# HGRN-2 values projected with tokens in the partitions, and the a-gate's product set beside the decays

## The chip, the core and the metric

The kernel runs on one core of a Trainium2 chip. A core has a matrix engine (TensorE, PE in the profile), which multiplies a stationary tile with a moving one into a PSUM bank, three engines for elementwise work (VectorE = DVE, ScalarE = ACT, GpSimd = POOL) and SyncE (SP), which starts DMA transfers. Each engine runs its own list of instructions in order; semaphores join them. The metric is the time of one execution on the device, in microseconds, the median of the runs. Loads of stationary tiles are a row of their own (PEld), which overlaps PE.

## What is computed

One layer of a diffusion backbone, for 1152 tokens (1024 latents and 128 context tokens) of width 1024. A normalised and modulated input goes through one input projection, `w_in`, whose columns feed two token mixers: HGRN-2 with four heads of 128, and RWKV-7 with eight heads of 64. An output projection and a gated ConvFFN follow. The change touches two places of the mixers:

```
def hgrn2_mixer(u_a, lb, norm_w, s0):
    q, i, zf, zb, g = jnp.split(u_a, 5, axis=-1)
    q = heads(jax.nn.silu(q))
    i = heads(i)
    f_f = lb[0] + (1 - lb[0]) * jax.nn.sigmoid(zf)
    f_b = lb[1] + (1 - lb[1]) * jax.nn.sigmoid(zb)
    o_f, S_f = hgrn2_chunk_scan(q, heads(1 - f_f), i, heads(jnp.log(f_f)), s0[:, 0])
...
def rwkv7_mixer(u_b, p, s0):
    u_b = dwconv1d(u_b, p['rwkv_conv'])
    r, k, v, wdf, wdb, ad, gd = jnp.split(u_b, idx, axis=-1)
    w_f = jnp.exp(-DECAY_SCALE * jax.nn.sigmoid(p['rwkv_w0'][0] + jnp.tanh(wdf) @ p['rwkv_w2'][0]))
    w_b = jnp.exp(-DECAY_SCALE * jax.nn.sigmoid(p['rwkv_w0'][1] + jnp.tanh(wdb) @ p['rwkv_w2'][1]))
    a = jax.nn.sigmoid(p['rwkv_a0'] + ad @ p['rwkv_a2'])
    kk = heads(k * p['rwkv_k_k']).astype(jnp.float32)
    k = k * (1 + (a - 1) * p['rwkv_k_a'])
```

`i` holds the HGRN-2 values, taken as they are, while q, both forget gates and g go through a nonlinearity. `a` is the a-gate of RWKV-7, `w_f` and `w_b` are its decays; each of the three is a product of inner size 32.

## The kernel before

**Products in three parts.** Inputs are fp32. The modulated input lies in SBUF as `hh` (rounded) and `hl` (the rest), with the 1024 channels in 8 groups of 128 partitions (`KT`) and the 1152 tokens in the columns. A weight column block is loaded into `wr` (512 KB; one buffer), `split` makes `wh` (a cast on ACT) and `wl` (the difference, on DVE; for the heads both carry the line of the call, L1229), and `proj` computes wh·hh + wh·hl + wl·hh: for each of three blocks of 384 tokens, 8 x 3 matmuls (L1070, L1071, L1072) of 128 stationary columns (the weights) by 384 moving ones (the tokens) into one of two banks, "pj". So a result has channels in its partitions and tokens in its columns. There are two buffers of `wh` and two of `wl`.

**HGRN-2's projections** (`hgrn_in`, L1225 to L1250): for each head in turn the blocks f, b, q and i, and at the end g of all heads. f, b, q and g go through Tanh to tiles "ha" and "hb" (two buffers each) and by DMA to DRAM. The value branch, `which == "i"`, turns the result round, since the scan needs tokens in the partitions: copy from the bank (L1234), three 128x128 transposes on PE (L1238) into another "pj" bank, copy again (L1239) and one store of 192 KB to `d_hv` (L1240). The scan loads the values of three token tiles from there at L1550 and L1650.

**RWKV-7's features** (`features`, from L1309, once for each of four head pairs, each in three blocks of 384 tokens): per block the a-gate's product from rows 64 to 95 of `wlora` and `twt` (`small_proj`, L1299, called at L1328) into a bank "sp", Tanh on ACT (L1331), the a-gate's use in `nb` and `k`; then the bonus sums (L1343), transposes of the values (L1353), and after these the two decays' products from rows 0 to 31 and 32 to 63 (L1364) into two banks "sp", with the decays' work behind them; last the products of pairs (L1397, L1398). Tag "sp" has two banks. Tag "el" has four places of 256 columns in the last two banks, and is used by `elim`.

**The eliminations** (`elim`, L1431): five of them, one behind each pair's features and one over all pairs; 31 steps of two DVE instructions each (L1441, L1444), then 32x32 products on PE (L1462, L1464). DVE does other work between the steps. The RWKV scan (its first product is L1713), the HGRN scan (L1582, L1608, L1627 and others), the output projection and the FFN (L2065, L2229) follow.

**What sets the order.** The Python code only records operations into a `Plan`. `close` finds what each depends on. Three tables written out in the file then decide: `SEQUENCE` the order in which the operations are issued (each engine's list is its part of it), `ENGINE_OF` the engine of every operation that has a choice (copies, combinations, stores: V, A, G, S), and `PLACE_OF` which buffer each tile takes. The remaining HGRN projections are spread by this order between the eliminations and into the scan.

## Time and profile before

| | |
|---|---|
| three runs | 1771.46, 1771.28, 1767.26 us; median 1771.28 |
| profiled execution | 1769.48 us, its span 1767.7 |
| TensorE clock granted, mean | 0.998 |
| DMA, whole span | 352.97 MB moved, mean 200 GB/s |
| start, to 40 us | loads, modulation, first columns |
| 40 to 487 us | projections, RWKV features, the eliminations |
| 487 to about 840 us | both scans, with projections between |
| about 840 to 1010 us | rest of the scans, output projection |
| 1010 to 1515 us | FFN up and its convolution |
| 1515 to 1768 us | FFN down |

The bounds of the stages are read from the lines that run in them. In the profile, "L1070 PE MATMUL banks<-hh,wh 128*128 128x384 f32 x768 | 278.5, 363 | 4.4" reads: line, engine, operation, tile written and tiles read, stationary tile (rows by columns), output (partitions by elements), count; then busy us and mean ns of one; then the idle time of the engine ahead of it, and what released it. A matmul's duration there reaches from its start to its modelled end, and consecutive ones overlap. `banks` is PSUM; `fx`, `low` and `top` are regions of SBUF that hold several tiles in turn ("ha", "hb" and `wlora` lie in `fx`, `twt` in `low`), so one name stands for several tiles.

### The profile page before, as it was taken

Reading aid. Unit: us, or ns where it says so; the run is one execution under the profiler, and the core shown is the slowest. Engines: PE = TensorE matmul, PEld = TensorE weight load, DVE = VectorE, ACT = ScalarE, POOL = GpSimd, SP = SyncE. Lnnn points to the kernel's source line nnn. Section 1 sums busy time; section 2 is a strip of 40 time slices with the busy share of each in tenths; the row PEclk is TensorE's granted clock in tenths of the full one; section 3 lists DMA queues with packets and bytes.
Section 4 is the critical chain, followed back from the end, with each engine's and each line's share of the span. In section 5 each row is a group of like instructions: output and inputs, shape, how many; then the busy total and the mean of one; then the engine's idle time right before and its main releaser. Section 6 shows DMA issues by size and latency. Waiting matters only on the chain.

```text
span 1767.7 us, 44608 instructions
## 1 busy us (share of the span) xinstructions
PE 1708.6 (97%) x17726; PEld 1539.8 (87%) x17726; DVE 1434.8 (81%) x2742; ACT 936.8 (53%) x1955; POOL 350.5 (20%) x543
## 2 busy tenths in 40 slices
PE   6999999999999999999999999999999999999998
PEld 4888888888988888888778899999999999878787
DVE  5648889977779988886879797888988888878766
ACT  5657576663255656664556764444444444554542
POOL 0003141352222011112110122232333322000000
PEclk9999999999999999999999999999999999999999
DMA  8426365486777788989997757777877777896775
GB/s 278 137 72 164 89 162 139 112 232 195 203 207 221 212 246 278 288 271 289 296 288 264 215 122 153 155 157 160 165 156 153 146 162 149 282 306 218 229 231 183
DMA packets 342068, 352.97 MB, mean 200 GB/s; under 512 B 73180, under 2 KB 264565, under 8 KB 341508
## 3 DMA queue, kind: packets, MB, share of 16 engines
q1 hardware_dynamic: 287508, 282.27, 53.0%
q0 software_dynamic: 54352, 67.85, 19.6%
q8 instruction: 139, 2.28, 0.5%
q14 instruction: 69, 0.57, 0.1%
HBM read 254.99 MB, written 118.10 MB: 211 GB/s over the span
## 4 chain that ended last, share of the span: by engine, by line
PE 55%; DVE 18%; DMA 15%; issue 5%; ACT 4%; SPq 1%; POOL 1%; DVEq 0%; ACTq 0%; POOLq 0%
PE banks L2065 14%; PE banks L1070 6%; PE banks L1072 5%; PE banks L1071 5%; PE banks L2229 5%; DVE low L2153 3%; DMA low<-in_ffn_w_up_dram 2%; DMA wr<-in_ffn_w_down_dram 2%; PE banks L1955 1%; PE banks L1957 1%; PE banks L1956 1%; DMA d_t<-in_ffn_w_down_dram 1%; DMA low<-d_a 1%; DMA wr<-in_ffn_w_up_dram 1%; DMA wr<-d_o 1%
## 5 line engine op out<-in xcount | busy, mean ns | idle before, releaser
L1070 PE MATMUL banks<-hh,wh 128*128 128x384 f32 x768 | 278.5, 363 | 4.4 <-DVE fx L1250 3.1
L1072 PE MATMUL banks<-hh,wl 128*128 128x384 f32 x768 | 257.8, 336 | 0.0
L1071 PE MATMUL banks<-hl,wh 128*128 128x384 f32 x768 | 257.5, 335 | 0.0
L2153 DVE SCALAR_TENSOR_TENSOR low<-low,pf 128x1024 f32<-128x1024 f32 x176 | 225.4, 1281 | 7.9 <-ACT low L2147 5.2
L2065 PE MATMUL banks<-qm,wh 128*128 128x320 f32 x968 | 224.1, 310 | 0.2 <-ACT fx L2102 0.2
L2065 PE MATMUL banks<-hbm,wh 128*128 128x256 f32 x880 | 164.4, 283 | 3.6 <-DVE low L2123 1.9
L2065 PE MATMUL banks<-qm,wl 128*128 128x320 f32 x528 | 162.9, 308 | 0.2 <-DVE wl L2035 0.2
L1070 PEld LDWEIGHTS banks<-hh,wh 128*128 128x128 f32 x768 | 144.3, 188 | 20.5 <-issue 8.5
L2065 PEld LDWEIGHTS banks<-qm,wh 128*128 128x128 f32 x968 | 160.7, 189 | 0.5 <-ACT fx L2102 0.4
L1071 PEld LDWEIGHTS banks<-hl,wh 128*128 128x128 f32 x768 | 144.6, 188 | 2.7 <-issue 1.4
L1072 PEld LDWEIGHTS banks<-hh,wl 128*128 128x128 f32 x768 | 144.2, 188 | 0.0
L2065 PEld LDWEIGHTS banks<-hbm,wh 128*128 128x128 f32 x880 | 139.1, 190 | 5.2 <-DVE low L2123 2.5
L2065 PE MATMUL banks<-ham,wh 128*128 128x256 f32 (+1 forms) x616 | 132.0, 294 | 0.0
L2065 PE MATMUL banks<-hbm,wl 128*128 128x256 f32 x440 | 124.4, 283 | 0.6 <-DVE wl L2035 0.6
L2102 ACT COPY fx<-banks 128x256 f32<-128x256 f32 (+1 forms) x132 | 52.1, 398 | 108.1 <-PE banks L2065 101.3
L2065 PEld LDWEIGHTS banks<-ham,wh 128*128 128x128 f32 x616 | 101.5, 190 | 0.1
L2065 PEld LDWEIGHTS banks<-qm,wl 128*128 128x128 f32 x528 | 99.1, 188 | 0.6 <-DVE wl L2035 0.6
L2065 PEld LDWEIGHTS banks<-hbm,wl 128*128 128x128 f32 x440 | 83.9, 191 | 0.8 <-DVE wl L2035 0.8
L2173 POOL DMA_DIRECT2D d_t<-in_ffn_w_down_dram x44 | 45.0, 1050 | 183.9 <-DMA d_t<-d_t 139.9
L2035 ACT CAST wh<-wr 128x512 fp32r<-128x512 f32 x73 | 45.2, 622 | 66.2 <-PE banks L2065 28.6
L2035 ACT CAST wh<-low 128x512 fp32r<-128x512 f32 x81 | 50.0, 620 | 52.9 <-PE banks L2065 25.5
L2065 PE MATMUL banks<-ham,wl 128*128 128x256 f32 (+1 forms) x264 | 77.0, 292 | 0.0
(578 smaller groups left out, 4369.3 us busy)
## 6 DMA issues: line engine op xcount, KB each, us to landing
wr<-in_w_in_dram SPq DMA_DIRECT2D x34, 512.0 KB
d_t<-in_ffn_w_down_dram POOLq DMA_DIRECT2D x61, 256.0 KB, 5.8
low<-d_a SPq DMA_DIRECT2D x53, 256.0 KB
low<-d_ak SPq DMA_DIRECT2D x64, 192.0 KB
low<-d_kb SPq DMA_DIRECT2D x36, 256.0 KB
low<-in_ada_w_dram SPq DMA_DIRECT2D x32, 256.0 KB
fx<-in_ada_w_dram SPq DMA_DIRECT2D x16, 512.0 KB
top<-in_ada_w_dram SPq DMA_DIRECT2D x16, 512.0 KB
```

The lines of the kernel that those rows point to most:

```text
L1070: mm(o, wh[:, kt, :], hh[:, kt, c], kt == 0, False)
L1071: mm(o, wh[:, kt, :], hl[:, kt, c], False, False)
L1072: mm(o, wl[:, kt, :], hh[:, kt, c], False, kt == KT - 1)
L1955: mm(ps, oh[:, kt, :], woh, kt == 0, False)
L1956: mm(ps, oh[:, kt, :], wol, False, False)
L1957: mm(ps, ol[:, kt, :], woh, False, kt == KT - 1)
L2035: split(*w, src)
L2065: pe.matmul(o, a[:, kt, :], b[:, kt, :], start=start and first, stop=last, skip_group_check=not start)
L2102: act.copy(keep[n], y[:, 0:w])
L2153: dve.scalar_tensor_tensor(av, shifted(dy, dx), tap(3 * dy + dx), av, MUL, ADD)
L2173: acc(td[j][k], b)
L2229: pe.matmul(o, x, y, start=fresh and f, stop=l, skip_group_check=not fresh)
```

## The change

Four parts.

- The HGRN-2 values are projected by a new function, `hgrn_rows`, for two heads at a time: the tokens are the stationary side (128 columns of `hh` or `hl`) and the weights of two heads the moving one (256 columns), so the result has tokens in its partitions. It takes nine token tiles of 8 x 3 matmuls (L1242, L1243, L1244 of the changed file). The weights come in two halves of four channel groups each, so that they fill both `wh` and both `wl` buffers. A result is copied from its bank once (L1246) and stored in two parts of 64 KB (L1248). The copies and transposes of the old branch are gone.
- The a-gate's product is taken in two halves of 192 columns into tag "el", and stands in one group with the two decays' products, at the start of the block (L1353, L1356); its Tanh goes in two halves as well (L1358).
- `close` counts what every alternative form of an operation reads, not the first alone, and the places of tag "el" may be taken in any order.
- The three tables are new throughout.

```
+    def hgrn_rows(h):
+        ws = []
+        for k0 in (0, 4):
+            raw = tl("wr", [P, 4, 256])
+            ld(raw, w_in[k0 * P:(k0 + 4) * P, 512 + h * P:512 + h * P + 256].rearrange("(a p) n -> p a n", p=P))
+            ws.append((tl("wh", [P, 4, 256], F32R), tl("wl", [P, 4, 256], F32R)))
+            split(*ws[-1], raw)
+        for i in range(NT):
+            o, c = pbank()[:, 0:256], slice(i * P, (i + 1) * P)
+            for kt in range(KT):
+                wh, wl = ws[kt // 4]
+                with plan.together():
+                    mm(o, hh[:, kt, c], wh[:, kt % 4, :], kt == 0, False)
+                    mm(o, hl[:, kt, c], wh[:, kt % 4, :], False, False)
+                    mm(o, hh[:, kt, c], wl[:, kt % 4, :], False, kt == KT - 1)
+            t = tl("hb", [P, 256])
+            copy(t, o)
+            for j in range(2):
+                st(hvd[h + j][:, i, :], t[:, P * j:P * j + P])
...
         for which in parts:
+            if which == "i":
+                hgrn_rows(h)
+                continue
...
-                if which == "i":
-                    copy(ta, ps)
-                    pv = pbank()
-                    with plan.together():
-                        for j in range(3):
-                            pe.transpose(pv[:, j * P:(j + 1) * P], ta[:, j * P:(j + 1) * P], ident)
-                    copy(tb_, pv[:, 0:384])
-                    st(hvd[h][:, 3 * tb:3 * tb + 3, :], tb_.rearrange("p (a b) -> p a b", b=P))
-                    continue
...
-            ps = small_proj(wlora[64:96, cb], twt[64:96, c])
-            act.activation(ta, ps, AF.Tanh, scale=0.5, bias=dp[:, D_A0H + p:D_A0H + p + 1])
+            dec = [pbank("sp")[:, 0:384] for d in range(2)]
+            al = [pbank("el", 256)[:, 0:192] for i in range(2)]
+            with plan.together():
+                for d in range(2):
+                    mm(dec[d], wlora[32 * d:32 * d + 32, cb], twt[32 * d:32 * d + 32, c], True, True)
+                for i in range(2):
+                    t0 = tb * 384 + 192 * i
+                    mm(al[i], wlora[64:96, cb], twt[64:96, t0:t0 + 192], True, True)
+            for i in range(2):
+                act.activation(ta[:, 192 * i:192 * i + 192], al[i], AF.Tanh, scale=0.5,
+                               bias=dp[:, D_A0H + p:D_A0H + p + 1])
...
-            dec = [pbank("sp")[:, 0:384] for d in range(2)]
-            with plan.together():
-                for d in range(2):
-                    mm(dec[d], wlora[32 * d:32 * d + 32, cb], twt[32 * d:32 * d + 32, c], True, True)
...
-    hin = iter([(h, w) for h in range(4) for w in "fbqi"] + [(h, "g") for h in range(4)])
+    hin = iter([(h, w) for h in range(4) for w in ("fbqi", "fbq")[h % 2]] + [(h, "g") for h in range(4)])
...
-        for m, a, k, _ in forms[0][1]:
-            w, r = self.operands(m, a, k)
-            writes += w
-            reads += r
+        for n, (_, l) in enumerate(forms):
+            for m, a, k, _ in l:
+                w, r = self.operands(m, a, k)
+                writes += [] if n else w
+                reads += r
...
-    plan.tag("el", [(mp, 512 * 6 + 256 * b) for b in range(4)], 256)
+    plan.tag("el", [(mp, 512 * 6 + 256 * b) for b in range(4)], 256, True)
...
-0 12 13 14 11 2 15 16 27 1 17 18 19 4 20 22 28 29 33 3 24 30 39 23 31 32 34 35 36 40 37 38
+11 27 28 29 0 1 17 12 2 30 18 19 33 39 13 14 15 20 4 3 16 21 22 23 24 25 31 32 34 35 36 37
```

The order on PE around the a-gate, in the second token block of the fourth head pair, before: the a-gate's product (L1299) stands by itself among projection matmuls and products of an elimination (L1462), with a group of transposes of the old value branch (L1238) two rows behind it; the names `wh_133` and `wl_136` are weight buffers with their numbers.

```order
L1072 MATMUL banks<-hh,wl_136 128x384
L1299 MATMUL banks<-low,fx 128x384
L1462 MATMUL banks<-top 32x32 x16
L1238 MATMUL banks<-c_ident,fx 128x128 x3
L1070 MATMUL banks<-hh,wh_133 128x384
```

The decays of the block (L1364) come 94 rows later, behind the transposes of the RWKV values, also among projections. In the changed kernel the products of a block stand in one group, here those of the same block, among matmuls of the new value projection (L1242 to L1244):

```order
L1242 MATMUL banks<-wh_133,hh 128x256
L1243 MATMUL banks<-wh_133,hl 128x256
L1244 MATMUL banks<-wl_136,hh 128x256
L1353 MATMUL banks<-low,fx 128x384 x2
L1356 MATMUL banks<-low,fx 128x192 x2
L1242 MATMUL banks<-wh_134,hh 128x256
```

The a-gate has moved into the decays' group, as two products behind two; the decays have moved ahead of the bonus sums and the transposes.

The order on PE where the first block of new value products begins: the last three matmuls of a projection of the old form (L1074 to L1076 are `proj` in the changed file) read weight buffers `wh_133` and `wl_136`, and twelve of the new form on the other two buffers follow, of which the first and the last three are shown; then comes the first that reads `wh_133` again, with other contents.

```order
L1075 MATMUL banks<-hl,wh_133 128x384
L1076 MATMUL banks<-hh,wl_136 128x384
L1242 MATMUL banks<-wh_134,hh 128x256
...
L1242 MATMUL banks<-wh_134,hh 128x256
L1243 MATMUL banks<-wh_134,hl 128x256
L1244 MATMUL banks<-wl_135,hh 128x256
L1242 MATMUL banks<-wh_133,hh 128x256
```

Before, a projection on the one pair of buffers ran for 72 matmuls while the other pair was filled; now both pairs are read in turn until nine token tiles are done.

The order on PE between the products of the fourth elimination and those of the fifth, before: 16 products of the fourth (L1464), a group of transposes, and then projections, the first of 240 in a row; further on the 16 first products of the fifth (L1462) stand ahead of another group of transposes.

```order
L1072 MATMUL banks<-hh,wl_136 128x384
L1464 MATMUL banks<-top,fx 32x32 x16
L1238 MATMUL banks<-c_ident,fx 128x128 x3
L1070 MATMUL banks<-hh,wh_134 128x384
...
L1072 MATMUL banks<-hh,wl_136 128x384
L1462 MATMUL banks<-top 32x32 x16
L1238 MATMUL banks<-c_ident,fx 128x128 x3
L1070 MATMUL banks<-hh,wh_133 128x384
```

In the changed kernel the last products of the fourth (L1488) are followed by projections of the old form, and those of the fifth (L1486) stand inside the second block of the new form:

```order
L1486 MATMUL banks<-top 32x32
L1488 MATMUL banks<-top,fx 32x32 x17
L1074 MATMUL banks<-hh,wh_134 128x384
...
L1244 MATMUL banks<-wl_135,hh 128x256
L1486 MATMUL banks<-top 32x32 x16
L1242 MATMUL banks<-wh_133,hh 128x256
L1243 MATMUL banks<-wh_133,hl 128x256
```

Between the two sets of products 240 matmuls of 384 columns have become 216 of them and 120 of 256 columns, and the transposes are gone.

55 lines of the change are left out of this document (28 added, 27 removed), and 602 rows, old and new, of the table SEQUENCE.

## The prediction

> **What bounds the kernel now.** I read the page's first part, then the busy times cut at four places of the program, then the chain of waits of one stretch, then single rows of the timeline.
>
> ```profile
> PE 1708.6 (97%) x17726; PEld 1539.8 (87%) x17726; DVE 1434.8 (81%) x2742; ACT 936.8 (53%) x1955; POOL 350.5 (20%) x543
> core 0: us, PE busy (x) PEld busy (x) DVE busy (x) ACT busy (x) POOL busy (x), PEclk, DMA share, GB/s
> 0.00:40.00 40.00, 24.38 (x156) 17.77 (x156) 21.35 (x61) 23.40 (x48) 4.09 (x20) 0.96 0.85 277
> 40.00:487.00 447.00, 439.16 (x4540) 395.05 (x4539) 351.19 (x715) 255.87 (x523) 116.39 (x218) 1.00 0.57 152
> 487.00:840.00 353.00, 340.09 (x6671) 300.27 (x6665) 295.65 (x734) 201.44 (x482) 62.72 (x120) 1.00 0.84 251
> 840.00:1010.00 170.00, 163.79 (x1597) 136.85 (x1594) 140.78 (x280) 101.83 (x222) 18.38 (x32) 1.00 0.86 271
> 1010.00:1515.00 505.00, 499.58 (x3716) 495.65 (x3716) 437.18 (x644) 235.35 (x458) 146.48 (x151) 1.00 0.74 156
> 1515.00:1768.00 253.00, 241.59 (x1064) 194.22 (x1062) 188.62 (x312) 118.88 (x228) 2.47 (x3) 0.99 0.73 238
> ```
>
> PE is busy in 98% of 40 to 487 us (projections, RWKV features, eliminations) and in 96% of 487 to 840 (scan, with the remaining HGRN projections as filler). The clock is full, so nothing is to be had there. The change works in these two stretches; the FFN and what follows it have the same products before and after, and I move them by nothing. DVE is second everywhere: 79% of the first stretch, 84% of the second, with 57 us idle in the latter. A busy PE is not a bound PE, so the second stretch is asked what its chain runs over.
>
> ```profile
> by line: PE banks L1070 7.4%; PE banks L1072 6.0%; PE banks L1071 5.9%; DVE top L1608 4.9%; PE banks L1627 4.3%; PE banks L1713 4.2%; DVE top L1607 4.2%; PE banks L1582 4.0%; PE banks L1767 3.7%; PE banks L1784 3.4%; PE banks L1760 3.4%; is
> L1070 PE MATMUL banks<-hh,wh 128*128 128x384 f32 x192 | 73.8, 384 | 0.0
> ```
>
> The three projection lines hold 19.3% of that chain, 68 us of 353. They issue 3 x 192 = 576 matmuls there, which at the interval below take 100 us. So about 68% of a filler matmul is on the path, and I count what leaves this stretch at 0.68.
>
> **The prices.** The mean of a matmul row (384 ns) is its latency; what the PE pays is the interval between starts.
>
> ```profile
> 440.12 0.33 PE L1071 MATMUL banks<-hl,wh 128*128 128x384 f32 x1
> ...
> 445.84 0.33 PE L1071 MATMUL banks<-hl,wh 128*128 128x384 f32 x1
> 1505.75 0.40 PE L2065 MATMUL banks<-hbm,wh 128*128 128x256 f32 x2
> ...
> 1507.19 0.40 PE L2229 MATMUL banks<-ham 128*128 128x512 f32 x1
> ```
>
> 33 intervals of 384 columns in 5.72 us are 0.1733 us each; 12 of 256 columns in the FFN, same type and a new stationary tile each time as in the new projection, take 1.44 us, 0.120 each.
>
> The value projection had 288 matmuls of 384 columns, 49.9 us, and gets 432 of 256, 51.8 us: **+1.9 us** for the same columns. The Trainium skill ("TensorE: Matmul & The Clock Gate", section "Back-to-back issue gap") gives N / 2.4 + 2.5 ns, by which the two forms would cost 46.8 and 47.2 us, so +0.4 as an estimate; the rows are 11 ns over it at both widths and decide.
>
> ```profile
> 343.81 0.49 PE L1238 MATMUL banks<-c_ident,fx 128*128 128x128 f32 x3
> 344.06 0.42 PE L1070 MATMUL banks<-hh,wh 128*128 128x384 f32 x1
> 344.32 0.33 PE L1071 MATMUL banks<-hl,wh 128*128 128x384 f32 x1
> 107.67 0.91 PE L1299 MATMUL banks<-low,fx 32*128 32x384 f32 x2
> 108.51 0.44 PE L1070 MATMUL banks<-hh,wh 128*128 128x384 f32 x1
> 108.79 0.34 PE L1071 MATMUL banks<-hl,wh 128*128 128x384 f32 x1
> 346.68 0.91 PE L1364 MATMUL banks<-low,fx 32*128 32x384 f32 x4
> 347.52 0.44 PE L1070 MATMUL banks<-hh,wh 128*128 128x384 f32 x1
> ```
>
> A group of three transposes holds the PE 0.25 us and stretches the next interval from 0.17 to 0.26: 0.34. At its other end stands the latency, 0.5; I take 0.45, since the matmul ahead is stretched too. Twelve groups go: -5.4 us.
>
> One a-gate product holds the PE 0.84 us and stretches the next interval to 0.28, so 0.94; twelve go, **-11.3 us**. The pair of decays takes 0.84 as well, as much as the one product alone, so products in different strips of 32 rows already run side by side. The a-gate's rows 64 to 95 are a third strip. Its two halves of 192 columns take half of 0.84 each, so both fit behind the decays: cost 0, between 0 and one half left over, 0.42 x 12 = 5.0. The Trainium skill (same page, section "The mechanism") says that matmuls start and end strictly in program order. By it a second half that waits for its strip may also hold back what follows, which is the upper end; no run here shows three strips at once.
>
> **Where they fall.** By the order of instructions, before and after: up to the last pair product of the features (381 us) the PE loses 75 projection matmuls (-13.0), 3 groups of transposes (-1.4) and all a-gate products (-11.3), and gets 216 value matmuls (+25.9): +0.2. From there to the first scan product (487 us) it loses 141 (-24.4) and 5 groups (-2.3) and gets 216 (+25.9): -0.8. Behind it 72 matmuls (-12.5) and 4 groups (-1.8) are missing: -14.3, at 0.68 **-9.7 us**.
>
> The middle piece isn't read from its sum, because two eliminations on DVE pace it.
>
> ```profile
> L1444 DVE TENSOR_TENSOR top<-top 128x31 f32<-128x31 f32 (+15 forms) x31 | 10.7, 344 | 1.0
> L1441 DVE TENSOR_TENSOR top<-top 128x31 f32<-128x31 f32 (+15 forms) x31 | 10.6, 343 | 0.9
> 420.81 1.08 PE L1462 MATMUL banks<-top 32*32 32x32 f32 x32
> 432.77 0.55 PE L1238 MATMUL banks<-c_ident,fx 128*128 128x128 f32 x3
> 475.10 0.63 PE L1462 MATMUL banks<-top 32*32 32x32 f32 x16
> 487.46 0.71 PE L1713 MATMUL banks<-low 64*128 64x128 f32 x8
> ```
>
> The fourth elimination fills 383 to 418 us on DVE: 21.3 us of its own, the rest other work between its steps (the two rows are of that stretch). Then come its products, the fifth elimination and its products. Filler ahead of the fourth's products: 198 matmuls before, 162 now, 6.2 us less, but DVE isn't faster, so I expect PE idle there instead: between -6.2 and 0, taken at 0. Inside its products 33 matmuls go: -5.7. Between them and the fifth's products (432.8 to 475.1 us) PE never pauses; 240 matmuls and a transpose group become 216 and 120 of the new ones: +37.4 +14.4 -41.6 -0.5 = +9.7. Inside the fifth's products 48 and two groups become 96 new ones: +11.5 -8.3 -0.9 = +2.3. Sum between +0.1 and +6.3. The upper end has DVE on the path; I take +2.5, below the middle of 3.2, since a DVE with less between its steps can end earlier.
>
> **What the new form adds.** Its weights lie in both weight buffers for nine token tiles. Where the first block of it begins, the second buffer has just been read by the last matmul of the old form.
>
> ```profile
> L1229 ACT CAST wh<-wr 128x1024 fp32r<-128x1024 f32 x20 | 21.0, 1048 | 6.1 <-PE banks L1071 3.3 <-DMA wr<-in_w_in_dram 2.7
> L1229 DVE TENSOR_TENSOR wl<-wr,wh 128x1024 fp32r<-128x1024 f32 x20 | 24.6, 1230 | 2.6 <-ACT wh L1229 2.4
> DMA to landing us min/median/max: 2.7/3.3/5.4
> L1234 ACT COPY fx<-banks 128x384 f32<-128x384 f32 x12 | 5.8, 480 | 20.6 <-PE banks L1072 16.6 <-DVE top L1441 4.0
> L1331 ACT ACTIVATE top<-banks,dp 128x384 f32<-128x384 f32 x12 | 6.9, 577 | 5.9 <-PE banks L1299 5.9
> ```
>
> Cast and difference take 2.3 us; 12 matmuls on the first buffer cover 1.4 of it. The wait is +0.8, with everything behind it on the in-order PE; at the second block 18 matmuls (2.2 us) come first, about 0. Bounds 0 to 3 for both, if ACT or DVE are late. At the end of both blocks the order puts other products or matmuls on the freed buffer first.
>
> A result tile is copied (some 0.4 us) and stored by two DMAs instead of one larger one; such stores landed in 3.3 us. With two tiles and a token tile every 24 x 0.12 = 2.9 us a tile has 5.8 us, so this hides: 0. If landing goes to its 5.4 us, each of 18 tiles is late by about 1 us; that end (+10, where the PE has nothing else) I give little weight, since both blocks have other products between.
>
> ACT loses 24 copies of 0.48 (11.5 us) and gets 16 smaller ones; its a-gate function goes in two calls of 192 columns instead of one of 0.577 us. ACT was half idle in both stretches, which hides this. Start, FFN and end keep their work: 0, within 3 either way, as their order is new too.
>
> **Sum** against the profiled execution's 1769.5 us (span 1767.7): +0.2 +0.8 +2.5 -9.7 = -6.2, so **1763 us**. The median of the three runs is 1771.3, 1.8 above that execution; I predict on the execution's scale.
>
> **The rivals.**
>
> *The scan stretch doesn't follow the PE.* Its chain also runs over the scan's own steps and DVE (L1607, L1608). If the filler only sat in gaps, -9.7 becomes about -2, and the time is 1771. Against it speaks the share of the projections on the chain, for it that PE waits were short but many. The same time comes out if the a-gate's halves aren't hidden (+5.0).
>
> *More comes through.* If all 14.3 us of the scan stretch and the -6.2 of the fourth elimination's filler count: 1763 - 4.6 - 8.7 = 1750.
>
> *Slower: DVE sets the pace.* The new order gives DVE more copies of the scan stretch.
>
> ```profile
> L1579 DVE COPY top<-top 128x384 f32<-128x384 f32 x12 | 4.3, 360 | 0.8 <-PE banks L1582 0.4 <-ACT top L1553 0.4
> L1817 DVE COPY top<-banks 64x256 f32<-64x256 f32 x12 | 5.0, 418 | 0.9 <-PE banks L1786 0.7
> ```
>
> L1579 goes from 12 to 20 there (+2.9), L1817 from 12 to 19 (+2.9), with L1601, L1762, L1769 and L1728 and less of L1628 some 10 us in all. If DVE is the limit, the scan stretch gets nothing from the PE and up to 10 us more; with the middle piece at +6.3 and the wait at 3 the time is 1769.5 + 0.2 + 3 + 6.3 + 10 = 1789 at most, 1779 with half of the copies on the path and the rest as in the sum. It decides once more than about 10 of DVE's 57 idle us lie where the scan can't use them. Against it: these are waits that mostly end on PE in the rows.
>
> **Chances.** Forecast (1757 to 1766) 0.47, more 0.12, no release or no hiding (within 0.3%, 1766 to 1776) 0.27, slower by DVE 0.14. A measurement of this kernel tells 0.3%, 5.3 us, from no change. A part of the forecast's own case lies near the edge, so: faster 0.57, same 0.28, slower 0.15. The range takes in the larger gain and the case without release, and leaves out a tenth on either side: 1750 to 1777; the likeliest case alone is 1757 to 1766.
>
> **What will show it.** Right: the new product's rows 0.12 us apart; the rows of the decays and the a-gate's halves within 0.9 us together; the first scan product at 487 to 493 us; the stretch from there to the FFN's first product 7 to 13 us shorter. Wrong: scan products not earlier against their first one, DVE above 90% there, or PE waiting for a weight split or a store at the new product's lines. A different length of the FFN or of the end by more than 3 us would mean that the new order matters more than the change of work.

## The result, and the profile after

The change made the kernel slower. The changed kernel takes 1786.05 us, median of five runs (1778.66 to 1788.16), against 1768.11 (five runs, 1765.78 to 1771.46) of the kernel before in the same session: ratio 1.0089, 95% interval 1.0071 to 1.0107 (the comparison's own estimate, not the quotient of the medians, which is 1.0101). The forecast was 1763 with a range of 1750 to 1777. The profiled execution took 1784.69 us (span 1782.9) at a mean granted clock of 0.991, against 1769.48 (1767.7) at 0.998.

The page's first part and the busy times cut at the same places as before (the columns are those of the table in the prediction):

```profile
PE 1708.3 (96%) x17858; PEld 1546.3 (87%) x17858; DVE 1437.5 (81%) x2779; ACT 915.1 (51%) x1931; POOL 375.5 (21%) x592
40.00:487.00 447.00, 429.85 (x4503) 392.52 (x4502) 346.20 (x717) 245.86 (x515) 121.50 (x233) 0.98 0.55 148
487.00:840.00 353.00, 326.84 (x6360) 286.57 (x6360) 286.72 (x711) 185.84 (x448) 77.65 (x144) 0.98 0.77 231
1515.00:1768.00 253.00, 253.00 (x1164) 208.94 (x1163) 201.64 (x329) 129.97 (x247) 8.05 (x12) 1.00 0.78 253
```

PE is as busy as before in all (1708), but in a longer span. The stretches are cut at the same times in both kernels, so they don't hold the same work. In the first two, PE has lost 9 and 13 us of busy time and the clock is no longer full. In the last one PE is never idle (253.0 of 253); before, it idled 11.4 us there, of which 6.8 lie behind its last product of FFN down.

Where the difference of 15.2 us arises is read from the first and last start of five lines that both kernels have: products of pairs (L1398, now L1422), first products of the RWKV scan (L1713, now L1737), first products of the output projection (L1955, now L1979), FFN up (L2065, now L2089), FFN down (L2229, now L2253). The view of one line gives the durations of a matmul (minimum, median, maximum, ns), then the first and last start. Before:

```profile
L1398 PE MATMUL banks<-top x576: 192/193/215, 137.9 to 381.3; 64*32 64x32 f32 x192
L1713 PE MATMUL banks<-low x576: 272/272/374, 487.5 to 923.8; 64*128 64x128 f32 x192
L1955 PE MATMUL banks<-ham,wh x72: 389/389/504, 869.7 to 994.8; 128*128 128x512 f32 x72
L2065 PE MATMUL banks<-qm,wh x968: 305/309/414, 1006.3 to 1505.5; 128*128 128x320 f32 x194
L2229 PE MATMUL banks<-qm x165: 277/392/499, 1515.2 to 1760.9; 128*128 128x512 f32 x153, 128*128 128x256 f32 x12
```

After:

```profile
L1422 PE MATMUL banks<-top x576: 186/193/259, 139.0 to 394.5; 64*32 64x32 f32 x192
L1737 PE MATMUL banks<-low x576: 272/272/419, 507.0 to 954.6; 64*128 64x128 f32 x192
L1979 PE MATMUL banks<-ham,wh x72: 389/389/504, 900.5 to 1021.4; 128*128 128x512 f32 x72
L2089 PE MATMUL banks<-qm,wh x968: 305/310/412, 1032.2 to 1525.4; 128*128 128x320 f32 x194
L2253 PE MATMUL banks<-qm,ham x78: 278/395/403, 1591.8 to 1775.2; 128*128 128x512 f32 x66, 128*128 128x256 f32 x12
```

| piece | before | after | difference | forecast |
|---|---|---|---|---|
| to the last product of pairs | 381.3 | 394.5 | +13.2 | +1.0 (+0.2, and 0.8 for the wait) |
| from there to the scan's first product | 106.2 | 112.5 | +6.3 | +2.5 (upper end +6.3) |
| from there to the FFN's first product | 518.8 | 525.2 | +6.4 | -9.7 |
| from there to the last product of FFN down | 754.6 | 743.0 | -11.6 | 0 |
| rest of the span | 6.8 | 7.7 | +0.9 | 0 |

Three pieces came out longer than the sum had them, and the FFN, which the sum left alone, came out shorter. The traces below show that two kernels with the same instructions in a piece can differ there by 8 to 10 us, so each difference is no better than that of two traces.

The prices that the sum was made of are confirmed, in the changed kernel's timeline of PE (start, duration, line, shape, count). The new value product, from the first block's start:

```profile
339.93 0.28 PE L1242 MATMUL banks<-wh,hh 128*128 128x256 f32 x1
...
340.88 0.28 PE L1244 MATMUL banks<-wl,hh 128*128 128x256 f32 x1
```

Eight intervals in 0.95 us are 0.119 each (forecast 0.120). The group of decays and a-gate halves:

```profile
103.54 0.33 PE L1076 MATMUL banks<-hh,wl 128*128 128x384 f32 x1
103.80 0.59 PE L1353 MATMUL banks<-low,fx 32*128 32x384 f32 x2
103.82 0.59 PE L1356 MATMUL banks<-low,fx 32*128 32x192 f32 x2
104.23 0.49 PE L1353 MATMUL banks<-low,fx 32*128 32x384 f32 x2
104.25 0.48 PE L1356 MATMUL banks<-low,fx 32*128 32x192 f32 x2
104.66 0.45 PE L1074 MATMUL banks<-hh,wh 128*128 128x384 f32 x1
```

The group holds the PE 0.86 us, the decays alone held it 0.84: the halves are hidden. Nor is the first value block's wait far off: PE waited 0.6 us for the difference on DVE there (forecast 0.8).

What the forecast did not have is the clock. Before, the granted clock halves only at the start and the end; after, it does so six times between 200 and 830 us, 27.3 us in all. The changed kernel's busy times, cut at the steps of the clock around the end of the fourth elimination:

```profile
421.59:425.00 3.41, 3.30 (x20) 2.98 (x18) 3.07 (x11) 0.00 (x0) 0.00 (x0) 1.00 0.90 282
425.00:428.42 3.42, 1.25 (x45) 1.09 (x49) 3.42 (x4) 0.93 (x3) 0.00 (x0) 0.99 0.01 2
428.42:431.83 3.41, 2.39 (x148) 2.11 (x143) 3.31 (x6) 1.87 (x4) 0.00 (x0) 0.50 0.32 120
431.83:435.24 3.41, 2.82 (x97) 2.61 (x86) 1.75 (x3) 0.00 (x0) 0.67 (x1) 0.50 0.55 154
435.24:438.66 3.42, 3.42 (x13) 3.42 (x12) 0.09 (x1) 0.56 (x1) 1.78 (x3) 0.51 1.05 269
```

What PE waited for in the second of these windows, in the view of waits (engine, tile and line, what it waited for, us in total, times, longest):

```profile
PE banks L1486 <- DVE top L1471: 1.4, 1, 1.4
PE banks L1486 <- ACT top L1497: 0.8, 1, 0.8
```

PE runs out of filler ahead of the products (L1486), waits 1.4 and 0.8 us, is busy 1.25 of 3.42 us, all of it in 32 x 32 products of the elimination, and gets half the clock for the next 10.24 us. A projection matmul then starts every 0.32 us (435.43, 435.75) instead of 0.17. The price of all six, in time of PE itself, is at most half of 27.3 us, since PE was not busy throughout.

### The profile page after: what moved, and what is told of

It reads as the page before. It is cut to its first block, busy times and chain, and to the rows that moved or that the text cites. A ratio compares the mean times of both kernels' runs of the same rounds, so it can differ in the third digit from the quotient of the medians.

```text
span 1782.9 us, 44799 instructions
## 1 busy us (share of the span) xinstructions
PE 1708.3 (96%) x17858; PEld 1546.3 (87%) x17858; DVE 1437.5 (81%) x2779; ACT 915.1 (51%) x1931; POOL 375.5 (21%) x592
## 4 chain that ended last, share of the span: by engine, by line
PE 55%; DVE 7%; DMA 7%; issue 3%; ACT 2%; SPq 1%; POOL 0%; DVEq 0%; ACTq 0%; POOLq 0%
PE banks L2089 24%; PE banks L2253 13%; PE banks L1979 2%; PE banks L1981 1%; PE banks L1980 1%; DMA d_hy<-top 1%; PE banks L1737 1%; PE banks L1074 1%; PE banks L1606 1%; PE banks L1808 1%; PE banks L1791 1%; DMA fx<-d_hf 1%; PE banks L1784 1%; PE banks L1076 1%; PE banks L1075 1%
## 5 line engine op out<-in xcount | busy, mean ns | idle before, releaser
L1074 PE MATMUL banks<-hh,wh 128*128 128x384 f32 x672 | 246.7, 367 | 5.8 <-ACT low L1298 2.7
L1076 PE MATMUL banks<-hh,wl 128*128 128x384 f32 x672 | 227.0, 338 | 0.0
L1075 PE MATMUL banks<-hl,wh 128*128 128x384 f32 x672 | 226.7, 337 | 0.0
L2089 PE MATMUL banks<-qm,wh 128*128 128x320 f32 x968 | 224.3, 310 | 0.6 <-ACT fx L2126 0.6
L2089 PE MATMUL banks<-hbm,wh 128*128 128x256 f32 x880 | 164.8, 282 | 1.1 <-ACT hbm L2019 0.5
L2089 PE MATMUL banks<-qm,wl 128*128 128x320 f32 x528 | 162.7, 308 | 0.0
L2089 PEld LDWEIGHTS banks<-qm,wh 128*128 128x128 f32 x968 | 160.5, 189 | 0.9 <-ACT fx L2126 0.8
L1074 PEld LDWEIGHTS banks<-hh,wh 128*128 128x128 f32 x672 | 127.7, 190 | 18.7 <-ACT low L1298 4.5
L2089 PEld LDWEIGHTS banks<-hbm,wh 128*128 128x128 f32 x880 | 139.7, 190 | 1.9 <-ACT hbm L2019 0.8
L2089 PE MATMUL banks<-ham,wh 128*128 128x256 f32 (+1 forms) x616 | 132.3, 294 | 0.0
L1075 PEld LDWEIGHTS banks<-hl,wh 128*128 128x128 f32 x672 | 128.2, 191 | 2.5 <-issue 1.4
L1076 PEld LDWEIGHTS banks<-hh,wl 128*128 128x128 f32 x672 | 127.3, 189 | 0.0
L2089 PE MATMUL banks<-hbm,wl 128*128 128x256 f32 x440 | 124.6, 283 | 0.4 <-DVE wl L2059 0.4
L2126 ACT COPY fx<-banks 128x320 f32<-128x320 f32 (+1 forms) x132 | 51.6, 398 | 119.7 <-PE banks L2089 109.4
L2089 PEld LDWEIGHTS banks<-ham,wh 128*128 128x128 f32 x616 | 101.5, 190 | 0.2
L2089 PEld LDWEIGHTS banks<-qm,wl 128*128 128x128 f32 x528 | 99.1, 188 | 0.3 <-DVE wl L2059 0.3
L2089 PEld LDWEIGHTS banks<-hbm,wl 128*128 128x128 f32 x440 | 83.9, 191 | 0.7 <-DVE wl L2059 0.6
L2197 POOL DMA_DIRECT2D d_t<-in_ffn_w_down_dram x44 | 50.3, 1204 | 127.7 <-DMA d_t<-d_t 82.8
L2089 PE MATMUL banks<-ham,wl 128*128 128x256 f32 (+1 forms) x264 | 77.0, 292 | 0.0
```

What stands on the lines that cost most here:

```text
L1074: mm(o, wh[:, kt, :], hh[:, kt, c], kt == 0, False)
L1075: mm(o, wh[:, kt, :], hl[:, kt, c], False, False)
L1076: mm(o, wl[:, kt, :], hh[:, kt, c], False, kt == KT - 1)
L2089: pe.matmul(o, a[:, kt, :], b[:, kt, :], start=start and first, stop=last, skip_group_check=not start)
L2126: act.copy(keep[n], y[:, 0:w])
L2197: acc(td[j][k], b)
```

## The experiments

Each result is a ratio to the kernel before, measured beside it, with its 95% interval; the changed kernel stands at 1.0089. Where an edit changes lines of the three tables, one pair of them is shown.

**Which stretch of the new order helps, and which harms.** *join_tail*: the kernel before, its order kept up to the first product of the output projection, the new order from there.

```
-5114 5361 5350 5138 5163 5159 5362 5050 5351 5164 5369 5370 5363 5364 5365 5378 5166 5379 5380 5381 5165 5410 5366 5411 5412 5413 5414 5013 5367 5149 5330 5415
+5114 5361 5350 5138 5163 5159 5362 5050 5351 5164 5157 5184 5151 5363 5364 5013 5410 5411 5412 4984 5369 5378 5379 5370 5365 5366 5367 5332 5333 5371 5372 5380
```

> The kernel before, its own order up to the first product of the output projection (before L1955), and from there the order of the changed kernel. The work is that of the kernel before throughout. From that product to the last product of the FFN the trace of before has 891.2 us (869.7 to 1760.9) and that of the changed kernel 874.7 (900.5 to 1775.2). If the new order of the tail is worth this by itself: 16 us less than before, about 1752 us. If the tail was only fast because the front was late (loads that had more time): no change, 1768.

Measured 1760.12 us (11 runs), 0.9956 [0.9936, 0.9975], faster than both kernels. Its rows of the output projection and of FFN down:

```profile
L1955 PE MATMUL banks<-ham,wh x72: 389/389/504, 875.8 to 997.2; 128*128 128x512 f32 x72
L2229 PE MATMUL banks<-qm,ham x78: 278/395/403, 1568.3 to 1752.2; 128*128 128x512 f32 x66, 128*128 128x256 f32 x12
```

The tail takes 876.4 us, against 891.2 before and 874.7 in the changed kernel, so the new order of the tail is worth about 15 us by these traces, and it needs neither of the two edits. But in four other traces the old order of the tail took 881.7 to 886.9 us (less_fill, less_front, scan_refill, front_new_scan_old, all below), and the time itself fell by 8.8 us: 5 to 15 is as close as the traces come.

It also shows what sets two traces apart. Up to the output projection this kernel issues what the kernel before issues, yet its scan took 390.6 us from its first product to there, against 382.2. Product by product it stays within 2.5 us of the trace before up to 826 us. Then its clock is halved for 6.8 us and it falls back by 3.3 us, and between 857 and 870 us by another 3:

```profile
826.00:833.00 7.00, 6.01 (x48) 5.42 (x44) 2.25 (x6) 1.00 (x3) 1.94 (x4) 0.59 1.05 321
```

*front_new_scan_old*: the changed kernel, its order kept up to the scan's first product, the old order behind.

```
-3014 2661 3026 3032 4620 4622 2662 2667 2668 2669 2670 2671 2672 3024 3020 2652 2653 4905 3004 3028 2677 2678 4621 3005 2673 3006 3076 2679 2680 3007 3077 3078
+3014 2661 3026 3032 4620 4622 2662 2667 2668 2669 2670 2671 2672 3024 3020 2652 2653 4905 3004 3028 2677 2678 4621 3005 2673 3006 2663 2674 2675 2664 3562 3560
```

> The changed kernel up to the first scan product, and from there the order of the kernel before (scan, output projection, FFN), with 72 matmuls of filler fewer than before in the scan. The first scan product should stand at 507 us as in the changed kernel. If the scan lost by its new order, it and the output projection take what they took before, 518.8 us, or up to 9.7 less, and with the old tail of 761 us the span is 1777 to 1787. If it lost by having less filler, whatever the order: 525 us or more, 1793 and up, with the clock again at half in places of the scan.

1.0146 [1.0114, 1.0178]. From the scan's first product to the FFN's it took 530.1 us, longer than either kernel, though the 72 value matmuls and four groups of transposes are gone from it. The clock was halved for 30.7 us there.

*less_fill*: the kernel before without 63 of the 72 matmuls of the fourth head's value projection, all in the scan.

```
+                if op.id in DROP: continue
...
+DROP = set([2695, 2696, 2697, 2698, 2699, 2700, 2701, 2707, 2708, 2709, 2710, 2711, 2712, 2713, 2719, 2720, 2721, 2722, 2723, 2724, 2725])
```

> The kernel before with 63 of the 72 matmuls left out in the value projection of the last head, which stands in the scan (groups 2 to 8 of every sum; these values are wrong then); its load, copies, transposes and stores stay, and so does every other place in the order. It removes 10.9 us of PE work from the scan. By the step of the forecast (0.68 of a filler matmul is on the path) it is 7.4 us faster than before, 1761. If the filler only lay in gaps: 1768 within 2. If it also kept the clock up: the trace has places at half clock in the scan that before hasn't, and the time is 1768 to 1775.

1.0017 [1.0, 1.0035]: 63 x 0.173 = 10.9 us of PE work less, and no gain. Two stretches of its scan:

```profile
600.00:610.00 10.00, 7.53 (x167) 6.18 (x167) 8.46 (x24) 3.87 (x12) 0.68 (x1) 0.73 0.78 239
630.00:640.00 10.00, 6.56 (x118) 5.63 (x119) 9.59 (x27) 4.09 (x13) 3.27 (x7) 0.66 0.88 272
```

and the same of the kernel before:

```profile
600.00:610.00 10.00, 9.70 (x198) 8.05 (x198) 9.43 (x25) 5.04 (x15) 1.59 (x3) 1.00 0.80 241
630.00:640.00 10.00, 8.75 (x145) 7.58 (x146) 9.01 (x26) 3.88 (x13) 2.88 (x6) 1.00 0.94 278
```

PE idles where the filler was, the clock is halved, and DVE and the transfers are no faster. From the scan's first product to the FFN's first its trace took 527.1 us, against 518.8, with 23.9 us at half clock. So the work that was left out did not come back as time. Whether the half clock took back a gain, this run alone doesn't tell.

*scan_refill*: front_new_scan_old with 72 matmuls of 384 columns whose result nobody reads, where the old value projection stood.

```
+    for _ in range(n):
+        for j in range(3):
+            plan.at(1)(partial(plan.units["PE"].matmul, o, w, x, start=j == 0, stop=j == 2))
```

> The run front_new_scan_old (changed kernel to the first scan product, then the old order) with useless products, 24 groups of three 128x384 as a projection has them, put into the 24 places of the old order that are empty there. It adds 12.5 us of PE work to the scan. If filler keeps the clock up and that is what the scan lacked: no fall of the clock in the scan, the stretch from the first scan product to the FFN's first product 519 to 523 us instead of 530, about 1788 (against 1797). If filler is work like any other: 535 to 542, 1802 to 1809.

1.0162 [1.0135, 1.0189]; the scan piece took 532.5 us. 12.5 us of PE work cost 2.4 us, and the halved clock went from 30.7 to 13.6 us, which can have paid for up to 8.5 us of that work. On balance filler cost little there, but restoring it doesn't restore the old scan.

*cover_all*: the changed kernel with 53 small matmuls of 128 columns, read by nobody, at 33 places where PE waits.

```
-                e, l = op.forms[0]
+                e, l = op.forms[0]; warm(self, op)
...
+    for _ in range(n):
+        plan.at(1)(partial(plan.units["PE"].matmul, o, i, i, start=True, stop=True))
```

> The changed kernel with 53 useless fp32 products of 128x128 (some 0.28 us each, 15 us in all) on PE, put directly ahead of the products that waited 0.4 us or more between 200 and 955 us in its trace. Nothing else is moved. If the halved clock is a cost of its own: the 27 us at half clock shrink to 10 or less and the time falls by 5 to 12 us in spite of the added work, to 1774 to 1781. If the clock only falls where PE has to wait anyway: no gain, 1786 within 3, or up to 10 more.

1.0112 [1.0089, 1.0135]: no gain. The scan piece in the changed kernel:

```profile
507.00:1032.00 525.00, 494.35 (x8137) 425.62 (x8136) 437.88 (x1035) 287.38 (x670) 98.56 (x181) 0.99 0.83 254
```

and with the small matmuls:

```profile
514.00:1034.00 520.00, 498.83 (x8200) 429.86 (x8199) 437.10 (x1035) 287.50 (x670) 100.46 (x181) 1.00 0.84 256
```

The clock stays full in the scan and the piece is 4.8 us shorter, but the front, where two falls of the clock were left, was 6.7 us later. The second of them came behind a window in which PE was busy for 3.11 of 3.41 us, most of it in 32 x 32 products:

```profile
430.23:433.64 3.41, 3.11 (x102) 2.67 (x102) 3.34 (x6) 2.14 (x5) 0.00 (x0) 1.00 0.02 5
```

The clock costs something; it isn't the whole.

**What the edits are worth.** *old_values*: the changed kernel with the old value branch, set into the slots of the new one.

```
-        for i in range(NT):
-            o, c = pbank()[:, 0:256], slice(i * P, (i + 1) * P)
...
+        for h in (h, h + 1):
+            w = load_w(w_in[:, 512 + h * P:512 + (h + 1) * P])
+            for tb, ps in proj(w, hh, hl):
...
```

> The changed kernel with its a-gate beside the decays and its order, but the values in the old form again: in the places of a block of the new form stand the two heads one after the other, each with its own weight buffer, 48 groups of three matmuls of 384 columns in the slots of 72 groups of 256, with the copies, transposes and stores of the kernel before. Theory A (the form is nearly free, the order loses the time): PE has 3.5 us more (5.4 for transposes, less 1.9), so 1786 to 1792. Theory B (weights in both buffers, 36 stores and two result tiles cost): 1772 to 1780.

1.0176 [1.0149, 1.0203], 0.9% (15 us; 13.7 by the medians) above the changed kernel. *apart*: the a-gate's halves in a group of their own, one row behind the decays.

```
+            with plan.together():
                 for i in range(2):
                     t0 = tb * 384 + 192 * i
```

> The changed kernel with the a-gate's two halves taken out of the group of the decays and put behind the next product of PE, so that they no longer stand directly beside them. By the trace a group of four takes 1.13 us and a group of two 1.11, and two halves alone would take about 0.84 more. If they were free only beside the decays and PE paces the front: the first scan product 8 to 11 us later (515 to 518), 1793 to 1797. If other work paces the front: 507 within 3, 1786.

1.0157 [1.0131, 1.0182], 0.7% (12 us; 10.9 by the medians) above. The rows of the same block now:

```profile
103.86 0.91 PE L1353 MATMUL banks<-low,fx 32*128 32x384 f32 x4
104.70 0.44 PE L1074 MATMUL banks<-hh,wh 128*128 128x384 f32 x1
...
105.42 0.91 PE L1357 MATMUL banks<-low,fx 32*128 32x192 f32 x4
106.27 0.45 PE L1074 MATMUL banks<-hh,wh 128*128 128x384 f32 x1
```

0.84 for the decays and 0.85 for the halves, 0.86 when they stand together. Both edits pay inside the new order. The order was made for them, so 15 and 12 us are upper readings.

*apart* also settles a question of the scan. From the scan's first product to the FFN's first it has the same instructions as the changed kernel on PE, DVE and ACT, but its clock is never halved there:

```profile
520.80:1042.70 521.90, 490.22 (x8138) 421.19 (x8137) 437.51 (x1035) 287.07 (x670) 100.76 (x181) 1.00 0.84 255
```

The changed kernel took 525.2 us, with 13.7 at half clock, so the falls cost it about 3 us in this piece. With a full clock the piece is still no shorter than with the old order (518.8 before, 522.8 in join_tail, 523.5 in less_front), though it holds 72 projection matmuls and four groups of transposes less, 14.3 us by the prediction's prices.

*old_order*: the new operations in the old order, the new operations put where the old ones stood. *values_alone*: the kernel before with the new value branch only, the old order shifted to make room. *values_tail*: values_alone with the new order of the tail.

```
-11 27 28 29 0 1 17 12 2 30 18 19 33 39 13 14 15 20 4 3 16 21 22 23 24 25 31 32 34 35 36 37
+0 12 13 14 11 2 15 16 27 1 17 18 19 4 20 22 28 29 33 3 24 30 39 23 31 32 34 35 36 40 37 38
...
-    hin = iter([(h, w) for h in range(4) for w in "fbqi"] + [(h, "g") for h in range(4)])
+    hin = iter([(h, w) for h in range(4) for w in ("fbqi", "fbq")[h % 2]] + [(h, "g") for h in range(4)])
```

> The changed kernel's work (values in the new form, a-gate beside the decays) in the order of the kernel before: each operation that both have stands at its old place, the blocks of projections fill the old slots one after the other, and what can't yet be issued waits for the next place. Theory A (the change itself is worth what was forecast; the new tables lose it, by thinner filler, waits and a halved clock): about 6 us less than before, 1762, clock 0.997 or more. Theory B (the new form costs by itself, by its weights in both buffers and its 36 stores, in any order): 1775 or more. Theory C (the steps of VectorE set the pace, the PE's work does not matter): 1768 within 3.

> The kernel before with the values in the new form and nothing else: its a-gate, its order and its tables, the blocks of projections one after the other in the old slots (26 us for a block of new values where one of the old took 12.5, the next ones later by as much, one block fewer behind), and what must wait for a weight buffer at the next place. The scan keeps as much filler as before (100 us of PE). PE has 3.5 us less (1.9 for the products, -5.4 for transposes). If the form itself is good: first scan product at 480 to 486 us, 1762 to 1767. If two weight buffers held for a whole block cost (the next weights come late): 1772 to 1785.

> The run above up to the first product of the output projection, and from there the order of the changed kernel, which gave 9 us in the kernel before (join_tail, 1760). If the two add up: 9 us less than the run above, 1750 to 1758 where that one is at 1762 to 1767, and the fastest kernel of all. If the tail's gain needs the front of before: as the run above.

1.091 [1.0884, 1.0936], 1.0715 [1.0688, 1.0741] and 1.066 [1.0632, 1.0688]. In old_order each pair of heads takes 10 to 13 us longer, from the first on (it ends at 175.4 us against 165.1), and the clock is halved for 158 us. values_alone is level with the kernel before until its first value block at 338 us. So the edits are worth nothing without an order of their own, and these three say little of the edits' own prices; values_tail repeats that the tail's gain (9 us) adds up.

**What makes the front late.** *less_front*: the kernel before without 63 matmuls of a value projection between 338 and 360 us (the same edit as less_fill, other numbers).

```
+DROP = set([2254, 2255, 2256, 2257, 2258, 2259, 2260, 2266, 2267, 2268, 2269, 2270, 2271, 2272, 2278, 2279, 2280, 2281, 2282, 2283, 2284])
```

> The kernel before with 63 of the 72 matmuls left out in the value projection of the first head (338 to 360 us, around the start of the third elimination's products; these values are wrong then). It removes 10.9 us of PE work ahead of the scan. By the forecast (PE paces the stretch to 381 us, one for one) the last pair product stands at 370 to 372 us; if that carries through, the first scan product is at 475 to 477 and the time 1758. If VectorE's eliminations pace the stretch: the first scan product at 483 to 487, 1765 to 1769.

1.0031 [1.0012, 1.005], and the last product of pairs is 3.6 us later, at 384.9. The place, in it:

```profile
340.00:360.00 20.00, 13.04 (x197) 10.21 (x198) 18.05 (x36) 10.81 (x22) 4.21 (x8) 0.68 0.40 110
```

and in the kernel before:

```profile
340.00:360.00 20.00, 19.92 (x260) 16.93 (x258) 19.46 (x39) 11.99 (x23) 6.17 (x12) 1.00 0.50 141
```

PE, full before, is idle for 7 us, chiefly for DVE at the bonus sums, and the clock is halved for 3.4 us at 343.8 us and for 17.1 from 350.6 us on. A PE that is 99% busy was not the only bound. The half clock can have taken back up to 10 us here.

*early_weights*: the weights of the projection behind the fourth elimination loaded and split earlier, and eight of its groups of three matmuls set ahead of the elimination's products. *ha_hb*: the new copies into two regions in turn, so that a copy waits less for a store.

```
-2164 2165 2107 2166 2167 2168 2169 2170 2171 2172 2173 2420 2421 2413 2414 2422 2423 2424 2174 2175 1899 2176 3133 2177 2178 3134 3135 2179 2180 2181 2182 2183
+2164 2165 2107 2166 2167 2168 2169 2170 2171 2172 2173 2420 2421 2413 2414 2422 2423 2424 2174 2175 1899 2176 3133 2177 2178 3134 3135 2179 2180 2463 2181 2182
...
-            t = tl("hb", [P, 256])
+            t = tl("hb" if i % 2 else "ha", [P, 256])
```

> The changed kernel with one place of its order mended: load, cast and difference of the weights that follow the fourth elimination stand ahead of its last steps instead of behind the first copies of its results, and the first 8 groups of that projection stand between its products, two ahead of each. No work is added or removed. If waits and the halved clock at 425 to 439 us are on the path: no fall of the clock there, the first scan product 5 to 9 us earlier (498 to 502), about 1779. If the fifth elimination's chain (loads, VectorE) sets the time there: the first scan product at 505 to 508, 1786.

> The changed kernel with the result tiles of the new values alternating between the tiles ha and hb (two buffers each) instead of hb alone, so that a copy waits for the store of four tiles before, not of two. Order and work are the same. In the changed kernel ACT waited 17.5 us for these stores between 434 and 507 us, PE 0.8 for the copies and 0.7 for another user of hb. If the stores delay what follows: 2 to 5 us less, 1781 to 1784. If they are hidden: 1786 within 2.

1.0123 [1.0097, 1.015] and 1.0113 [1.0087, 1.0138]: no gain from either. With the weights early the clock still fell at 430.8 us, for 6.8 us. Stores of the new values cost nothing that matters, as forecast.

*dve_light*, *pe_light*, *both_light*: the changed kernel without the two DVE differences of the first value block; without 63 of its matmuls; without both.

```
+DROP = set([2252, 2255])
...
+DROP = set([2268, 2269, 2270, 2271, 2272, 2273, 2274, 2279, 2280, 2281, 2282, 2283, 2284, 2285, 2290, 2291, 2292, 2293, 2294, 2295, 2296])
```

> The changed kernel without the two differences of the first value block's weights on VectorE (its wl holds older numbers, the values of two heads are wrong). In the trace they take 1.2 us each inside the third elimination, and the second waits 2.2 us for its buffer: the elimination should end at about 352 instead of 356.5 us. If VectorE sets the place of the third elimination's products: first product 4 to 5 us earlier (355 to 356), last pair product at 390, and as much at the first scan product. If PE's work ahead of it does: 360 within 1.5, first scan product 507 within 2.

> The changed kernel without 21 of the 48 groups of new values that stand ahead of the third elimination's products (three token tiles keep one group of eight; values wrong): 7.6 us of PE work less. If PE sets the place: first product of the third elimination at 353 to 356 (VectorE's end at 356.5 allows no more than about 2 us less than 360.5 unless it ends earlier too). If VectorE does: 358.5 to 360.5, PE waits, and the clock falls at about 355.

> The two runs above in one. If both set the place, each hiding the other: first product of the third elimination at 353 to 356, more than the two single gains together, the last pair product at 386 to 389. If the clock falls instead: no more than the better of the two.

1.0103 [1.0077, 1.0129], 1.0122 [1.0098, 1.0147], 1.0129 [1.0103, 1.0155]. The third elimination's first product came at 360.2, 362.1 and 362.3 us, against 360.5 in the changed kernel and 350.7 before. Without the differences DVE waits at another step:

```profile
DVE low L1304 <- ACT low L1300: 4.0, 1, 4.0
```

Without the matmuls the clock is halved at 349.1 us for 10.2 us.

*third_first*: the last 24 steps of the third elimination set back to back on DVE, ahead of other work, and its products earlier. *third_fifth*: also a transfer of the fifth elimination (L1450) earlier, and two multiplications (L1269) behind it.

```
-1841 2254 1842 1843 1844 1845 1846 1847 2255 2256 2257 1945 1944 2258 2259 2260 1946 2261 2262 2263 2267 2268 2269 2270 2271 1689 1463 1769 2264 2266 1947 1771
+1841 2254 1842 1843 1844 1845 1846 1847 1848 1849 1850 1851 1852 2255 1853 1854 1855 1856 1857 1858 1859 1860 1861 1862 1863 1864 1865 1866 1867 1868 1869 1870
...
-3138 3064 2446 2447 2448 1902 2452 2453 2195 2196 2197 2198 2199 2200 2201 2202 2203 2204 2205 2206 2207 2208 2210 2454 1911 2463 1904 2455 2456 2457 2458 2459
+3138 2142 3064 2446 2447 2448 1902 2452 2453 2195 2196 2197 2198 2199 2200 2201 2202 2203 2204 2205 2206 2207 2208 2210 2454 1911 2463 1904 2455 2456 2457 2458
```

> The changed kernel with the last 24 steps of the third elimination moved ahead of the convolution and feature steps that VectorE had in front of them (5 of them ahead of the weight difference that waited 2.2 us), and its first products on PE moved ahead of 20 groups of new values, the bonus sums behind them. No work is added or removed. The third elimination should end at about 348 instead of 356.5 us and its first product stand at 351 to 353 instead of 360.5. If this order is what makes the front late: the last pair product at 386 to 390 and the first scan product at 498 to 503, about 1779. If PE's total work and its waits elsewhere set the front: the first scan product at 505 to 510, 1786.

> The run above, and in the fifth elimination: the store of the context system goes out 30 us earlier (its load, and so the fifth elimination's start, waited for it), and the copy that waited 5.4 us for a store stands 14 elimination steps later. If VectorE's order makes the front late: the fifth elimination ends 5 to 9 us earlier than in the run above and the first scan product is at 492 to 498, about 1772. If PE sets the place: the first scan product as in the run above, within 2.

1.0105 [1.0072, 1.0139] and 1.014 [1.0097, 1.0183]. In third_first the elimination is as short as before (31.9 us on DVE, from 40.0) and its first product comes at 353.1 us, 7.4 us earlier; but its last one comes at 385.6 (380.2 in the changed kernel) and the last product of pairs at 400.0 (394.5). The gain was gone within 33 us. In third_fifth the first product of the fifth elimination came at 501.9, later than the 492.0 of the changed kernel.

## Why the prediction was wrong, step by step

**"The clock is full, so nothing is to be had there."** The sentence is true of the kernel before, but it was taken as a constant, and none of the rivals let it fall. The schedule keeps the clock full with filler; a change of the filler's places can lose it. Six falls between 200 and 830 us cost PE at most 13.6 us. How much of the 15.2 us they really make isn't settled: without those of the scan that piece was 3.3 us shorter in apart and 4.8 in cover_all. The Trainium skill ("TensorE: Matmul & The Clock Gate", section "What's actually happening") says that the clock halves after at least one idle window of about 3.4 us, in windows that run free of the program. The step of 3.41 us and the factor of two agree. That the window must be idle does not. The one shown held 1.25 us of 32 x 32 products only, but in early_weights the clock fell at 1215.86 us behind a window with 1.19 us of full-size FFN matmuls and one wait of 2.2 us:

```profile
1212.45:1215.86 3.41, 1.19 (x8) 0.93 (x8) 2.70 (x5) 1.98 (x4) 0.00 (x0) 1.00 1.08 276
```

Nor does the busy share decide it: in cover_all 3.11 of 3.41 us didn't keep the clock. What counts as activity these traces don't show.

**"So about 68% of a filler matmul is on the path."** This is the step that failed in the scan (-9.7 forecast, +6.4 measured). A share of the chain of waits says through which work the chain runs, not what comes back when that work goes: less_fill took 63 such matmuls out of the old scan and gained nothing, scan_refill put 72 in at 2.4 us. Both moved the clock too, but apart, with the new scan at a full clock, has 14.3 us less of PE work and is no shorter than the old one. The first rival, that the scan stretch doesn't follow the PE, had the mechanism right, and ended at about -2. The remaining rise is smaller than it looks: the old scan up to the output projection took 382.2 us in the trace of before and 390.6 and 389.4 in two kernels that issue the same instructions there (join_tail, less_front), and 393.5 in the changed kernel. So 3 to 11 us of rise, part of it spread and about 3 of it the clock's.

**+0.2 to the end of the features.** Here the same fallacy: matmuls were counted at their interval, as if PE were the only bound of that piece. less_front speaks against it: 10.9 us of PE work less, and 3.6 us later, though part of that can be the half clock's.

Where the 13.2 us arise, the ends of the four pairs tell: they come 0.8, 1.6, 2.2 and 13.2 us later than before, and by the sum's own prices they should have come at -3.9, -5.1, -7.4 and +0.2. So most of the step in the fourth pair is work that the sum had placed there (216 value matmuls for 81 projection matmuls), and what it missed is spread: 4.7 us in the first pair, 2.0 to 3.3 in each of the others. The start isn't it: the first matmul starts 3.8 us later (7.1 against 3.3 us), but the first one of `proj` only 0.4 (73.4 against 73.0 us).

By kind, summed from each matmul's start to the next one's: from the last product of the first pair to that of the fourth PE takes 228.6 us against 216.2, +12.4, where the terms of the sum give +4.0 (+4.8 with the wait): projections -10.6 (forecast -12.0), values +28.0 (+25.9), transposes -0.9 (-1.4), a-gate and decays with other products of that kind -4.7 (-8.5), pairs +1.2, others -0.6 (0 each). Every kind is worse by a little, because intervals hold the waits too; no single one carries it. Two of the twelve groups of decays and a-gate show such a wait plainly: they held the PE 1.82 and 2.39 us (at 134.8 us, still in the first pair, and at 272.5).

**+2.5 in the middle piece.** It came at its stated upper end, +6.3, by other terms. The 6.2 us of filler ahead of the fourth elimination's products, taken at 0, did come through (-7.7 from the last product of pairs to the first of the fourth elimination: 31.8 us against 39.5), and with them came the idle PE that halved the clock. The piece between the fourth's and the fifth's products was to grow by 9.7 us and grew by 15.4 (57.9 against 42.5). PE was busy for 55.7 of the 57.9 us: 2.2 us of idle time, and 4.5 us at half clock, which cost up to 2.3, make up most of the 5.7 us that the sum missed. DVE's fifth elimination took 43.5 us instead of 35.3, with two waits for transfers in it:

```profile
DVE fx L1269 <- DMA d_hf<-fx: 5.4, 1, 5.4
DVE top L1872 <- DMA top<-d_g: 1.8, 1, 1.8
```

But it ended 5.5 us ahead of its products (2.8 before), and moving work out of it, third_fifth, didn't shorten the piece (63.2 us).

**"Start, FFN and end keep their work: 0, within 3 either way."** -11.6 us in the FFN by these two traces. In the four other traces with the old order of the tail the FFN took 747.8 to 752.1 us, so 5 to 12 us are the new order's. The same work in a new order was worth about as much as both edits' forecast; the prediction had named a different length of the FFN as the sign that "the new order matters more than the change of work", and gave it no price. What waits went, from the waits of PE behind 1035 us, the four longest before:

```profile
PE banks L2065 <- DVE low L2123: 1.9, 2, 1.1
PE banks L2065 <- ACT fx L2102: 1.5, 3, 0.7
PE banks L2229 <- ACT qm L2211: 1.3, 2, 0.7
PE banks L2229 <- DVE qm L2211: 1.2, 4, 0.5
```

and after:

```profile
PE banks L2089 <- ACT fx L2126: 0.6, 1, 0.6
PE banks L2089 <- ACT hbm L2019: 0.5, 1, 0.5
PE banks L2089 <- DVE hbm L2019: 0.5, 1, 0.5
PE banks L2089 <- DVE wl L2059: 0.4, 1, 0.4
```

**The prices of the edits were right**: 0.119 us for 0.120, hidden halves for hidden halves, 0.6 for 0.8, stores that cost nothing. **The rival on the slower side** (DVE sets the pace, 1779 to 1789) gave the right time for the wrong reason: it asked for DVE above 90% in the scan, and there it was busy 437.9 of 525 us, 83%.

**What stays open** is which wait sets the pace of the front. Late weights, stores, the differences on DVE, the value matmuls, the place of the third elimination's steps and the transfer of the fifth were each changed alone and none brought time back. Either several are level with each other, so that each hides the next, or it is one that wasn't tried; the runs don't tell these apart. Nor was the new order run with both edits undone.

## What to carry to other kernels

In a schedule that is filled to 98%, work taken out doesn't come back at its price: removing 10.9 us of filler gave no time at two places, while separating a hidden product cost 12 us; test "does this stretch follow that engine" by leaving work out of the old kernel before counting on it. An order searched for one set of operations is part of the price of every edit, and a new one moves stretches that the edit doesn't touch: compare piece by piece, and keep the pieces that gained. Here that is the tail alone, 1760 us, faster than either kernel.

## What the runs showed that was not expected

- The clock halves in steps of 3.41 us, and it can do so after a window in which PE was busy for a third (1.25 of 3.42 us in small products, 1.19 of 3.41 in full-size ones), with no wait longer than 1.4 and 2.2 us. It did so even after 3.11 busy of 3.41 us, most of it in 32 x 32 products. Removed filler sets it off: less_front was at half clock for 17.1 us in a row, where the kernel before had it full.
- Products in three strips of 32 rows run side by side: two of 384 columns and two of 192 hold the PE 0.86 us, the two alone 0.84, the halves alone 0.85.
- The same instructions can take 382.2, 389.4 and 390.6 us in three profiled executions of three kernels that agree in that stretch, so a piece of one trace is not good to 5 us. In join_tail, 3.3 us of this came in one fall of the clock.
